# A hybrid decoder step: w_out, cq and co as seven half-size products, with the residual kept scaled and one weight queue behind the mixers

## The chip, the core and the metric

The kernel runs on one core of a Trainium2 chip. TensorE (PE) multiplies, VectorE (DVE) and ScalarE (ACT) do elementwise work, SyncE (SP) issues every DMA of this kernel, and GpSimd (POOL) does next to nothing. The metric is the device time of one launch in microseconds (us).

## The reference, cut to what matters

All is fp32. 512 prompt tokens and 8 decode tokens go through one layer with 2048 channels; both share the weights, so the kernel handles them as 520 columns.

```python
h  = rmsnorm(x, g_mix)
z  = h @ w_in                                   # 2048 -> 5128
y  = concat(rmsnorm(RG_LRU(z)) , headnorm(mLSTM(z)) * sigmoid(og))
x += y @ w_out
q  = rmsnorm(x, g_xattn) @ w_cq                 # 4 heads of 512
mk, mv = rmsnorm(mem, g_mem) @ w_mk, @ w_mv     # 256 memory tokens
x += softmax(q mk^T / sqrt(512)) mv @ w_co      # decode tokens: cached K, V of their own
x += relu(rmsnorm(x, g_ffn) @ w_up)^2 @ w_down  # 2048 -> 8192 -> 2048
out = rmsnorm(x, g_final)
```

## The kernel before

**Layout.** Channels lie on the 128 partitions and tokens in the columns: T is 520, HT half of it (260), and each activation is 16 tiles (k-tiles) of 128x520. Every fp32 product is three products of a shorter format: a weight is split into `whi` (a cast on ACT) and `wlo` (a subtraction on DVE), an activation likewise, and hi·hi, hi·lo and lo·hi are added in PSUM.

**The job list.** The mixers, w_out, w_cq, w_mk/w_mv and w_co are one list `jobs` of weight granules of 512 KB (8 k-tiles of 128x128). `run_jobs` takes them in order: job i+3 is loaded (`w_load`, L98), job i+2 is split (`w_split`, L105 on ACT, L106 on DVE), small generators in `tasks` are stepped by the job's cost, job i is multiplied (`gemm`, L157, 48 matmuls of 260 columns per granule), and its result is taken from PSUM. w_out, w_cq and w_co have 32 jobs each, so 1536 matmuls each; w_mk and w_mv have 64 together. Since the list runs on through all stages, the weights of the next stage are loaded and split while the one before still multiplies.

**Stages in the list.** `residual` (w_out and w_co) loads a tile of x (L699), adds the PSUM result (L705), stores the sum to DRAM (`dx`, L706), splits it as the operand of what follows (`xatt`), and adds up the squares; the norm itself is one row of factors (`rssx`, `rssf`) that is made behind the last tile by a small matmul (L208) and a Newton step (L198 to L201). `ev_q` (L726) multiplies the q tiles by that row. `attn_decode_all` is a task: per head and decode token it loads a broadcast q row and two K tiles of 256 KB, reduces them on DVE (L775), and later does the same with V (L802). It advances two steps per job in w_cq, and 0.7 steps in w_mk/w_mv (`DRATE` 2.0, `MCOST` 0.35). `attn_prompt` is started per head when its mk is there. Everything stays in SBUF, in 66 `slots`.

**Behind the list.** `ffn` closes all pools, and `prepare` loads x back, multiplies it by the norm (L1075, L1077), builds the eight column sums and halves that the fast product wants (`mixed`, L972 to L974), spills them to DRAM (L977), and reloads them as seven operand sets (`operand`, L983 to L986). From there each 2x2 block of weights (a unit: two output tiles, all of K in two halves) is done as **seven products of half size**, each of 24 matmuls of 260 columns (`product`, L1059) instead of eight. Four raw granules and three sums of them (L1025, four DVE operations) feed the seven products; each is split (L1040, L1041). There are 32 units for up and four groups (d1 to d4) of 8 for down; the results of up (L1093 to L1108) are spilled as the operands of down, and `down_evac` (L1118) adds products to x. At the end of a group the last unit frees one operand set per product and the next group's set is loaded and split into its place. Between up and down the weight pool is replaced, so no weight is loaded ahead there. The final norm stands at L1177 to L1193.

**Queues.** SP alone issues DMAs, in program order, and the DMAs take eight semaphores in turn, so a DMA also waits for the eighth one ahead of it. A DMA that waits for its data holds back all loads that stand behind it.

Of the kernel before, what the change touches and what calls it, by code (L numbers as in the profile page):

```python
# [19 lines left out]
NB = 8  # L20
# [7 lines left out]
SLOTS = 66  # L28
# [11 lines left out]
MCOST = 0.35  # L40
# [3 lines left out]
def tile_trunk(ctx: ExitStack, tc: tile.TileContext, a, o):  # L44
# [4 lines left out]
    keep = ctx.enter_context(tc.tile_pool(name="keep", bufs=1))  # L49
    part1 = ctx.enter_context(ExitStack())  # L50
    const = part1.enter_context(tc.tile_pool(name="const", bufs=1))
    slots = part1.enter_context(tc.tile_pool(name="slots", bufs=SLOTS))
    wpool = part1.enter_context(tc.tile_pool(name="wpool", bufs=3))
    small = part1.enter_context(tc.tile_pool(name="small", bufs=2))
    pmm = part1.enter_context(tc.tile_pool(name="pmm", bufs=2, space=PSUM))
# [35 lines left out]


# [8 lines left out]
    def w_split(i):  # L101
        raw = jobs[i].pop("raw")
        hi = wpool.tile([P, 8, P], F32R, tag="whi", name=nm("whi"))
        lo = wpool.tile([P, 8, P], F32R, tag="wlo", name=nm("wlo"))
        S.copy(hi, raw)  # L105
        V.tensor_tensor(out=lo, in0=raw, in1=hi.bitcast(F32), op=ALU.subtract)  # L106
        jobs[i]["w"] = hi, lo
# [141 lines left out]
    ident = const.tile([P, P], F32, name="ident")  # L249
# [11 lines left out]
    od = const.tile([P, 16, NB], F32, name="od")  # L261
    rmc = const.tile([P, 2], F32, name="rmc")
    rssf = keep.tile([P, T], F32, name="rssf")
    drows = dram.tile([4, 3, TP], F32, name="drows")

    st = {}
    xact, y = [], []
# [14 lines left out]
    def prologue():  # L282
# [9 lines left out]
        for k, x in enumerate(xs):  # L292
            g = pc(C_MIX, k)
            hi, lo = slot("xh", dt=F32R), slot("xl", dt=F32R)
# [18 lines left out]
    def rstd_task(key, n=D):  # L313
        yield
        st["r" + key] = rstd_of(st[key], n, "r" + key, rssf if key == "ssf" else None)
# [12 lines left out]
    def early_task():  # L328
        st["rssq"] = rstd_of(st["ssq"], D, "rssq")
        yield  # L330
        for ev, t in early:
            ev(halves(t))
# [156 lines left out]
    def ml_prompt(h):  # L489
# [102 lines left out]
        r = rstd_of(sq, 256, "rh")  # L592
        for j in range(2):
# [27 lines left out]
    def rnn(i, xc):  # L621
# [41 lines left out]
        if i == 7:  # L663
            yield
            yield
            rr = rstd_of(st["ssr"], 1024, "rr")
            for i in range(8):
# [4 lines left out]
                y.append(split(hg[i], "yr"))  # L672


    ym = []

    def ev_og(i):
        def ev(ps):
# [4 lines left out]
            ym.append(split(hm[i], "ym"))  # L683
            if i == 7:
                assert not tasks and len(y) == 8
                y.extend(ym)
# [62 lines left out]
    def attn_decode(h):  # L749
# [27 lines left out]
        for _ in range(4):  # L777
            yield
# [552 lines left out]
```

## Time and profile before

| | |
|---|---|
| median of three runs | 2898.87 us (2893.91, 2899.44, 2898.87) |
| the profiled execution | 2893.72 us, span 2892.0 us |
| mean granted TensorE clock | 0.973 |
| moved by DMA | 464.38 MB, 161 GB/s over the span |
| w_out on TensorE | 624.0 to 808.2 us |
| w_cq | 808.2 to 996.6 us |
| w_mk and w_mv with the attention | 996.7 to 1243.0 us |
| w_co | 1243.0 to 1433.4 us |
| gap with `prepare`, then up and down | 1433.4 to 1491.6 us, then to 2864.7 us |

The profile gives busy time per engine, and for each wait what ended it. A stage in which PE is busy all the time is bound by its matmuls; where PE is idle, the wait that ended last there is the price. A windows view gives, for a stretch of time, its length, the busy time of PE, PE weight loads, DVE, ACT and POOL with their instructions in brackets, the granted PE clock as a share of full speed, the busy share of the DMA engines, and GB/s.

### The profile page before, as it was taken

Reading aid. Unit: us, or ns where it says so; the run is one execution under the profiler, and the core shown is the slowest. Engines: PE = TensorE matmul, PEld = TensorE weight load, DVE = VectorE, ACT = ScalarE, POOL = GpSimd, SP = SyncE. Lnnn points to the kernel's source line nnn. Section 1 sums busy time; section 2 is a strip of 40 time slices with the busy share of each in tenths; the row PEclk is TensorE's granted clock in tenths of the full one; section 3 lists DMA queues with packets and bytes.
Section 4 is the critical chain, followed back from the end, with each engine's and each line's share of the span. In section 5 each row is a group of like instructions: output and inputs, shape, how many; then the busy total and the mean of one; then the engine's idle time right before and its main releaser. Section 6 shows DMA issues by size and latency. Waiting matters only on the chain.

```text
span 2892.0 us, 51735 instructions
## 1 busy us (share of the span) xinstructions
PE 2717.2 (94%) x21558; PEld 2662.7 (92%) x21558; DVE 2001.2 (69%) x3098; ACT 1225.0 (42%) x1620; POOL 31.3 (1%) x32
## 2 busy tenths in 40 slices
PE   7999999999999999999829999999998989999996
PEld 7999999999999988899829999999997989989896
DVE  7677687743346676733267777777778787887886
ACT  3444555632242244432225455454554343443543
POOL 3000000000000000000000000000000000000001
PEclk9999999999999999999959999999999999999998
DMA  4445442334448777744284544545456353433532
GB/s 149 144 164 169 163 140 86 96 103 139 135 152 269 271 250 253 227 139 133 91 291 161 163 160 156 168 141 169 154 183 224 102 191 110 155 139 109 190 106 81
DMA packets 198947, 464.38 MB, mean 161 GB/s; under 512 B 22349, under 2 KB 72173, under 8 KB 198713
## 3 DMA queue, kind: packets, MB, share of 16 engines
q1 hardware_dynamic: 198712, 461.08, 47.8%
q8 instruction: 169, 2.77, 0.4%
q14 instruction: 66, 0.53, 0.1%
HBM read 391.64 MB, written 69.49 MB: 159 GB/s over the span
## 4 chain that ended last, share of the span: by engine, by line
PE 77%; DMA 9%; DVE 9%; issue 2%; ACT 2%; SPq 1%; DVEq 0%; ACTq 0%
PE mm L157 29%; PE acca L1059 23%; PE accc L1059 12%; PE accb L1059 6%; PE mm L858 2%; DMA kv<-in_K 2%; PE aux L176 2%; DMA kv<-in_V 2%; PE mm L887 1%; DVE wlo L106 1%; DMA ct<-in_C 1%; DMA opl<-td 1%; DVE opl L986 1%; DVE wlo L1041 1%; DMA tdx<-w 1%
## 5 line engine op out<-in xcount | busy, mean ns | idle before, releaser
L1059 PE MATMUL acca<-oph,whi 128*128 128x260 f32 x2048 | 585.4, 286 | 63.6 <-ACT whi L1040 59.3
L1059 PE MATMUL acca<-opl,whi 128*128 128x260 f32 x2048 | 586.5, 286 | 13.5 <-DVE opl L986 13.1
L1059 PE MATMUL acca<-oph,wlo 128*128 128x260 f32 x2048 | 583.4, 285 | 3.2 <-DVE wlo L1041 3.0
L105 ACT CAST whi<-wraw 128x1024 fp32r<-128x1024 f32 x242 | 253.4, 1048 | 604.4 <-PE mm L157 382.8
L1059 PEld LDWEIGHTS acca<-oph,whi 128*128 128x128 f32 x2048 | 389.1, 190 | 66.7 <-ACT whi L1040 61.2
L106 DVE TENSOR_TENSOR wlo<-wraw,whi 128x1024 fp32r<-128x1024 f32 x242 | 298.2, 1233 | 189.7 <-ACT whi L105 187.8
L1059 PEld LDWEIGHTS acca<-opl,whi 128*128 128x128 f32 x2048 | 389.8, 190 | 17.1 <-DVE opl L986 17.1
L1040 ACT CAST whi<-raw 128x1024 fp32r<-128x1024 f32 x256 | 268.6, 1051 | 303.4 <-PE acca L1059 133.7
L1059 PEld LDWEIGHTS acca<-oph,wlo 128*128 128x128 f32 x2048 | 391.0, 191 | 4.4 <-DVE wlo L1041 4.3
L1041 DVE TENSOR_TENSOR wlo<-raw,whi 128x1024 fp32r<-128x1024 f32 x256 | 312.3, 1220 | 51.7 <-ACT whi L1040 51.3
L1040 ACT CAST whi<-raws 128x1024 fp32r<-128x1024 f32 x192 | 201.2, 1048 | 303.7 <-PE accc L1059 109.9
L1041 DVE TENSOR_TENSOR wlo<-raws,whi 128x1024 fp32r<-128x1024 f32 x192 | 234.7, 1222 | 114.3 <-ACT whi L1040 114.0
L1059 PE MATMUL accc<-oph,whi 128*128 128x260 f32 x1024 | 292.7, 286 | 5.6 <-ACT whi L1040 3.2
L1059 PE MATMUL accc<-oph,wlo 128*128 128x260 f32 x1024 | 291.5, 285 | 4.0 <-DVE wlo L1041 4.0
L1059 PE MATMUL accc<-opl,whi 128*128 128x260 f32 x1024 | 292.6, 286 | 0.8 <-DVE opl L986 0.6
L157 PE MATMUL mm<-xh,whi 128*128 128x260 f32 x1312 | 275.0, 291 | 10.9 <-DVE xh L295 10.7
L157 PE MATMUL mm<-xl,whi 128*128 128x260 f32 x1312 | 268.6, 286 | 5.6 <-DVE xl L296 5.5
L157 PE MATMUL mm<-xh,wlo 128*128 128x260 f32 x1312 | 268.9, 286 | 0.3 <-DVE wlo L106 0.3
L157 PEld LDWEIGHTS mm<-xh,whi 128*128 128x128 f32 x1312 | 207.5, 192 | 13.5 <-ACT whi L105 6.2
L157 PEld LDWEIGHTS mm<-xl,whi 128*128 128x128 f32 x1312 | 205.8, 191 | 7.8 <-DVE xl L296 7.8
L157 PEld LDWEIGHTS mm<-xh,wlo 128*128 128x128 f32 x1312 | 206.3, 192 | 0.7 <-DVE wlo L106 0.6
L1059 PEld LDWEIGHTS accc<-oph,whi 128*128 128x128 f32 x1024 | 194.4, 190 | 7.2 <-ACT whi L1040 4.4
(371 smaller groups left out, 5695.5 us busy)
## 6 DMA issues: line engine op xcount, KB each, us to landing
raw<-in_w_up SPq DMA_DIRECT2D x128, 512.0 KB
raw<-in_w_down SPq DMA_DIRECT2D x128, 512.0 KB
wraw<-in_w_in SPq DMA_DIRECT2D x80, 512.0 KB
td<-w SPq DMA_DIRECT2D x32, 1040.0 KB
opl<-td SPq DMA_DIRECT2D x56, 520.0 KB
wraw<-in_w_out SPq DMA_DIRECT2D x32, 512.0 KB
wraw<-in_w_cq SPq DMA_DIRECT2D x32, 512.0 KB
kv<-in_K SPq DMA_DIRECT2D x64, 256.0 KB
```

Source lines behind the costliest of these rows:

```text
L105: S.copy(hi, raw)
L106: V.tensor_tensor(out=lo, in0=raw, in1=hi.bitcast(F32), op=ALU.subtract)
L157: PE.matmul(ps[:, hf, 0:HT], w[:, j, :], x[:, HALF[hf]], start=(k == 0 and wi == 0), stop=(k == n - 1 and wi == 2))
L176: PE.matmul(out, u, v, start=first and i == 0, stop=last and i == 2)
L858: PE.matmul(box["ps"], w[:, i, :], x, start=(k == 0 and wi == 0), stop=(k == KB - 1 and wi == 2))
L887: PE.matmul(box["ps"][:, i], x[:, ms], w[:, j], start=(k == 0 and wi == 0), stop=(k == KB - 1 and wi == 2))
L986: V.tensor_tensor(out=lo, in0=lo.bitcast(F32), in1=hi.bitcast(F32), op=ALU.subtract)
L1040: S.copy(hi, raw)
L1041: V.tensor_tensor(out=lo, in0=raw, in1=hi.bitcast(F32), op=ALU.subtract)
L1059: PE.matmul(out, w[:, k], x[:, j], start=(new and k == 0 and i == 0), stop=(k == 7 and i == 2), skip_group_check=not new)
```

## The change

`rest` replaces everything behind the mixers, `ffn` among it.

- w_out, w_cq and w_co become 8 units each of seven half-size products, like up and down: 1344 matmuls each, not 1536. Their weights are packed in DRAM as w_up's (`pairs`). w_mk and w_mv keep their matmuls (`plain`, 64 granules).
- One list `seq` holds the products of all stages, and one weight queue (`sources`, `fetch`, `prep`, 7 raw tiles) runs through it, also from up to down: a product is prepared two ahead (`LOOK`).
- The operands of each product are seven sets with all sums, spilled to DRAM (`td`) as they are made and reloaded by `set_load`, a set as soon as the last unit of the stage before has freed its place. For the last of eight k-pairs `set_tail` splits straight from SBUF. The mixers spill theirs in `pair_out`.
- Norms move. The residual x is multiplied by the first norm's row (`scl`) in `scale_x` while the mixers run, and what is added to it carries the same factor, so that the norm of the attention is applied to q only (`r1`, and `esc` stands for the epsilon). The MLP needs none in front, since relu² scales with the square of its input: x is scaled back instead (`up_enter`, `scale_back`).
- The memory tokens' norm and gain are made in the mixers (`mem_prep`, to DRAM) and reloaded as w_cq's operand sets fall free (`mem_load`). q goes to DRAM and comes back per head in `attn_prompt`. K and V are packed for 512-KB loads with 4 KB per partition, where before 256 KB had 2 KB (K) or 1 KB (V) each.
- The decode attention is stepped 0.4 times per product of w_cq and twice per granule of w_mk and w_mv.
- `SLOTS` falls from 66 to 36.

The diff, cut to its core. First the mixers' side (`scale_x`, the factors, `pair_out`) and what the residual of before was:

```diff
+    def scale_x():
+        for n in range(KB):
+            x = slot("xs")
+            load(x, a["xT"][n])
+            yield
+            yield
+            V.tensor_tensor(out=x, in0=x, in1=scl, op=ALU.mult)
+            load(dx[0][n // 2][:, n % 2], x)
...
-        yield
+        st["rssq"] = rstd_of(st["ssq"], D, "rssq", scl)
+        V.scalar_tensor_tensor(out=esc, in0=scl, scalar=EPS, in1=scl, op0=ALU.mult, op1=ALU.mult)
+        yield
+        start(scale_x())
+        start(mem_prep(), 0.2)
...
+    def pair_out(k, ya, yb):
+        ta, tb = slot("ta"), slot("tb")
+        (a0, a1), (b0, b1) = ([t[:, c] for c in HALF] for t in (ya, yb))
+        (t1, t3), (t2, t4) = ([t[:, c] for c in HALF] for t in (ta, tb))
+        for out, in0, in1 in ((t1, a1, a0), (t3, b1, a1), (t2, b1, t1), (t4, b0, t2)):
+            V.tensor_tensor(out=out, in0=in0, in1=in1, op=ALU.subtract)
+        d = td["out"][k // 4]
+        load(d[:, 0:2, k % 4], halves(ya))
+        load(d[:, 4:6, k % 4], halves(ta))
+        load(d[:, 3, k % 4], b0)
+        load(d[:, 2, k % 4], b1)
+        load(d[:, 6:8, k % 4], halves(tb))
...
-    def residual(wname, acts, src, dst, gain, key, out):
...
-            def ev(ps, n=n, box=box):
-                if n == 0:
-                    st[key] = slot(key)
-                x1 = slot("x1")
-                V.tensor_tensor(out=halves(x1), in0=ps, in1=halves(box["x"]), op=ALU.add)
-                load(dst[n], x1)
-                if out is not None:
-                    out.append(split(x1, "xa", pc(gain, n)))
-                add_sq(st[key], x1, n == 0)
-                if n == KB - 1:
-                    start(rstd_task(key))
-            js += gemm([a[wname][n, g] for g in range(2)], acts, ev, pre)
-        return js
```

Then the core of `rest`: operand sets, the weight queue, the residual, q and the decode attention, the ends of the stages, and the loop over `seq` (what stood behind the last product of before, `final`, keeps its form):

```diff
+        def set_load(key, s, last=4):
+            out = []
+            for b, n in ((0, 4), (1, last)):
+                hi, lo = op_tile(), op_tile()
+                load(lo[:, 0:n].bitcast(F32), td[key][b][:, s, 0:n])
+                S.copy(hi[:, 0:n], lo[:, 0:n].bitcast(F32))
+                lo_of(lo[:, 0:n], lo[:, 0:n].bitcast(F32), hi[:, 0:n])
+                out.append((hi, lo))
+            sets[key, s] = out
+        def set_tail(key, j, wa, wb=None):
+            for _, _, s in ORDER:
+                src = wa[:, s] if wb is None or s < 4 else wb[:, s - 4]
+                hi, lo = sets[key, s][1]
+                S.copy(hi[:, j], src)
+                lo_of(lo[:, j], src, hi[:, j])
...
+        def fetch(k, q):
+            if k < len(sources):
+                t = praw.tile([P, 8, P], F32, tag="raw", name=nm("raw"))
+                load(t, sources[k][q])
+                raws[k, q] = t
+        def prep(n):
+            if n < len(seq):
+                ws[n] = split_weights(seq[n]["prep"]())
+        A11, A21, A22, A12, SS = range(5)
...
+        def strassen(key, n, src, evac, enter_=None, leave=None, left=None):
+            for u in range(n):
+                k = len(sources)
+                sources.append([src(u, i, j) for i, j in ((0, 0), (1, 0), (1, 1), (0, 1))])
+                box = {}
+                for p in range(7):
+                    job = dict(unit=k, q=p, cost=0.2, prep=lambda k=k, p=p: weights(k, p),
+                               run=lambda w, p=p, box=box: product(key, p, w, box),
...
+                    st_["w"] = w
+                    if u < 7:
+                        spill(nxt, u, w)
+                    load(dx[dst][u], X)
+                    if u == 0:
+                        st_["ss"] = tl("ss", (P, 2, T))
+                        S.activation(flat(st_["ss"]), flat(X), AF.Square)
+                    else:
+                        sq = tl("sq", (P, 2 * T))
+                        S.activation(sq, flat(X), AF.Square)
+                        V.tensor_tensor(out=flat(st_["ss"]), in0=flat(st_["ss"]), in1=sq, op=ALU.add)
...
+                V.tensor_tensor(out=t[:, 2], in0=t[:, 2], in1=r[:, 1], op=ALU.mult)
+                V.tensor_tensor(out=t[:, 3], in0=t[:, 3], in1=r[:, 0], op=ALU.mult)
+                h, j = u // 2, 2 * (u % 2)
+                d = dq32[h]
+                load(d[:, j], flat(t[:, 0:2]))
+                load(d[:, j + 1, 0:HT], t[:, 3])
+                load(d[:, j + 1, HT:T], t[:, 2])
...
+        def attn_decode(h):
...
+            def fetch(b, rows, n, src):
+                q, t = tl("qb", (P, 512)), tl("kv", (P, 1024))
+                load(q[:, 0:n], rows_of(rows, b * n, n))
+                load(t, src[h, b].rearrange("p a b -> p (a b)"))
+                return q, t
+            cur = [fetch(b, dqd[h], 512, a["K"]) for b in range(2)]
+            for b in range(NB):
+                yield
+                qb, kt = cur.pop(0)
+                for i in range(2):
...
+        def mem_load(s):
+            k4 = len(mact) // 4
+            if k4 < 4:
+                hi, lo = op_tile((P, 4, NMEM)), op_tile((P, 4, NMEM))
+                load(lo.bitcast(F32), dmem[:, 4 * k4:4 * k4 + 4])
+                S.copy(hi, lo.bitcast(F32))
+                lo_of(lo, lo.bitcast(F32), hi)
+                mact.extend((hi[:, j], lo[:, j]) for j in range(4))
...
+        def att_left():
+            while tasks:
+                step_tasks()
+            for _, _, s in ORDER:
+                set_load("co", s, 3)
+            set_tail("co", 3, *wlast)
...
+        def up_enter():
+            enter("d", t=2, w=2, x=2, r=1)()
+            v, s_ = tl("t", (P, 2, T))[:, 0], tl("t", (P, 2, T))
+            mean_of(v)
+            st["rphi"] = tl("r", (P, T))
+            V.reciprocal(s_[:, 0], v)
+            V.reciprocal(s_[:, 1], scl)
+            V.tensor_tensor(out=st["rphi"], in0=v, in1=s_[:, 1], op=ALU.mult)
+            V.tensor_tensor(out=scl, in0=scl, in1=s_[:, 0], op=ALU.mult)
+            start(scale_back())
...
+        def plain(srcs, run, post):
+            for q0 in range(0, len(srcs), 4):
+                k = len(sources)
+                sources.append(srcs[q0:q0 + 4])
+                for q in range(4):
+                    seq.append(dict(unit=k, q=q, cost=1.0, prep=lambda k=k, q=q: raws[k, q],
+                                    run=lambda w, g=q0 + q: run(g, w), post=lambda g=q0 + q: post(g)))
```

```diff
...
+        for n, j in enumerate(seq):
+            if "enter" in j:
+                j["enter"]()
             with tc.high_priority(offset=AHEAD):
...
+                if j["q"] < 4:
+                    fetch(j["unit"] + 1, j["q"])
+                prep(n + LOOK)
+            step_tasks(j["cost"])
+            j["run"](ws.pop(n))
...
```

**SP, from the mixers to w_out.** Rows give line, operation, what is written from what, and shape. Before, the weights of w_out (`wraw`) are loaded among those of the mixers, and its own evacuations come between them:

```order
L98 DMA wraw_6911<-in_w_in 128x1024
L98 DMA wraw_6973<-in_w_in 128x1024
L98 DMA wraw_7028<-in_w_out 128x1024
L98 DMA wraw_7090<-in_w_out 128x1024
L98 DMA wraw_7145<-in_w_out 128x1024
L98 DMA wraw_7207<-in_w_out 128x1024
L98 DMA wraw_7264<-in_w_out 128x1024
L98 DMA wraw_7327<-in_w_out 128x1024
L98 DMA wraw_7384<-in_w_out 128x1024
L706 DMA dx_0_100<-x_1002_7319 128x520
L699 DMA xr_7454<-in_xT 128x520
L98 DMA wraw_7448<-in_w_out 128x1024
```

Now the last pair of the mixers is spilled (`hh`, `ta`, `tb` to `tdout`), x is fetched for the first units, and the four raw weights of the first unit and the first operand set (`op`) stand behind that:

```order
L713 DMA tdout_109<-tb_7186 128x2x260
L709 DMA tdout_109<-hh_4081 128x2x260
L928 DMA x_7579<-dx_0_124 128x1040
L928 DMA x_7811<-dx_1_125 128x1040
L710 DMA tdout_109<-ta_7408 128x2x260
L711 DMA tdout_109<-hh_4082 128x260
L712 DMA tdout_109<-hh_4082 128x260
L713 DMA tdout_109<-tb_7409 128x2x260
L844 DMA raw_7446<-in_w_out 128x1024
L844 DMA raw_7448<-in_w_out 128x1024
L844 DMA raw_7450<-in_w_out 128x1024
L844 DMA raw_7452<-in_w_out 128x1024
L824 DMA op_7455<-tdout_108 128x1040
```

The loads that w_out begins with have moved from the mixers' stretch to behind the last head's spills, with the first operand set behind them.

**DVE, in the w_mk and w_mv stage.** Before, the decode attention's K reductions (L775) stand in some of the gaps between weight splits (`wlo`), with the prompt attention of a head (`mk`, `qa`) in others:

```order
L106 TENSOR_TENSOR wlo_11670<-wraw_11632,whi_11669 128x1024
L186 TENSOR_TENSOR mkl_11737<-mk_11519,mkh_11736 128x512
L106 TENSOR_TENSOR wlo_11701<-wraw_11667,whi_11700 128x1024
L775 ISA kv_11600,sc_11250<-kv_11600,kv_11599 128x512
L775 ISA sc_11250 128x1
L865 TENSOR_TENSOR mk_11664<-mm_11673,rm_9932 128x256
L775 ISA kv_11601,sc_11250<-kv_11601,kv_11599 128x512
L775 ISA sc_11250 128x1
L106 TENSOR_TENSOR wlo_11733<-wraw_11698,whi_11732 128x1024
L186 TENSOR_TENSOR mkl_11741<-mk_11664,mkh_11740 128x512
L186 TENSOR_TENSOR qal_11745<-q_9266,qah_11744 128x512
L106 TENSOR_TENSOR wlo_11780<-wraw_11730,whi_11779 128x1024
```

Now two K reductions (L1035; where V is due, four of L1054) stand in each gap:

```order
L98 TENSOR_TENSOR wlo_11796<-raw_11706,whi_11795 128x1024
L1035 ISA kv_11624,sc_11622<-kv_11624,qb_11623 128x512
L1035 ISA sc_11622 128x1
L1035 ISA kv_11624,sc_11622<-kv_11624,qb_11623 128x512
L1035 ISA sc_11622 128x1
L1095 TENSOR_TENSOR op_11566<-mk_11768,rm 128x256
L98 TENSOR_TENSOR wlo_11832<-raw_11750,whi_11831 128x1024
L1035 ISA kv_11628,sc_11622<-kv_11628,qb_11627 128x512
L1035 ISA sc_11622 128x1
L1035 ISA kv_11628,sc_11622<-kv_11628,qb_11627 128x512
L1035 ISA sc_11622 128x1
L818 TENSOR_TENSOR op_11836<-op_11566,op_11835 128x1024
```

Four splits of before have one pair of reductions among them, in their three gaps; now every gap has its pair, each on a load of 512 KB of its own and a broadcast row (`qb`).

**DVE, at the end of w_co.** Before, the last sum of squares (`ssf`) is followed by the norm's row (L209 to L201) and then `prepare` (L1075, L1077), with nothing of the next product between:

```order
L705 TENSOR_TENSOR x_2179_15902<-mm_15801,xr_15799 128x520
L220 TENSOR_TENSOR ssf_14267<-ssf_14267,sq_15905 128x520
L705 TENSOR_TENSOR x_2183_16007<-mm_15910,xr_15908 128x520
L220 TENSOR_TENSOR ssf_14267<-ssf_14267,sq_16010 128x520
L209 TENSOR_SCALAR rssfv_16013<-aux_16014 128x260
L209 TENSOR_SCALAR rssfv_16013<-aux_16017 128x260
L199 TENSOR_TENSOR rssft_16021<-rssfs_16020 128x520
L200 SCALAR_TENSOR_TENSOR rssft_16021<-rssft_16021,rssfv_16013 128x520
L201 SCALAR_TENSOR_TENSOR rssf<-rssft_16021,rssfs_16020 128x520
L1075 SCALAR_TENSOR_TENSOR w_16054<-xs_16051,par,rssf 128x260 x2
```

Now the splits of up's operand sets (L818: `op` from `op` for seven k-pairs, `op` from `w` for the last) and up's first weights (`wlo`, sums `raws`) stand among the last additions (`x`), and the two reciprocals of `up_enter` come between them:

```order
L818 TENSOR_TENSOR op_16085<-w_16241,op_16084 128x260
L798 TENSOR_TENSOR raws_16210<-raw_16089,raws_16210 128x1024
L818 TENSOR_TENSOR op_16123<-op_16123,op_16122 128x1040
L98 TENSOR_TENSOR wlo_16377<-raw_16006,whi_16376 128x1024
L818 TENSOR_TENSOR op_16128<-w_16241,op_16127 128x260
L961 SCALAR_TENSOR_TENSOR t_16298<-ax_16276,esc 128x260
L961 SCALAR_TENSOR_TENSOR t_16298<-ax_16279,esc 128x260
L1198 RECIPROCAL t_16299<-scl 128x520
L818 TENSOR_TENSOR op_16128<-op_16128,op_16127 128x780
L818 TENSOR_TENSOR op_16162<-op_16162,op_16161 128x1040
L818 TENSOR_TENSOR op_16167<-w_16241,op_16166 128x260
L1197 RECIPROCAL t_16299<-t_16298 128x520
```

The reload through a separate stage is gone; its place is taken by operand splits, weight splits and 520-column reciprocals in one row.

More of the change, by code (lines that the diff above doesn't have):

```diff
@@ L1198, in w_in @@
+        final()
+        stage["stack"].close()
+        whole.close()
     def w_in(n):
```

829 lines of the change are left out of this document (405 added, 424 removed).

## The prediction

> **What bounds the kernel now.** I read the page first: the share of each engine, and the share of the chain of waits that ended last.
>
> ```profile
> PE 2717.2 (94%) x21558; PEld 2662.7 (92%) x21558; DVE 2001.2 (69%) x3098; ACT 1225.0 (42%) x1620; POOL 31.3 (1%) x32
> PE 77%; DMA 9%; DVE 9%; issue 2%; ACT 2%; SPq 1%; DVEq 0%; ACTq 0%
> ```
>
> TensorE is busy for 94% of the span and holds 77% of the chain: matmuls bound the kernel, DMA and VectorE hold 9% each. Those are averages, so I cut the span by stage: mixers, w_out, w_cq, w_mk/w_mv, w_co.
>
> ```profile
> 45.00:624.00 579.00, 565.51 (x4540) 557.96 (x4539) 414.26 (x902) 288.05 (x460) 1.99 (x9) 0.98 0.40 129
> 624.00:808.20 184.20, 184.20 (x1538) 184.20 (x1537) 70.34 (x79) 52.12 (x64) 0.00 (x0) 1.00 0.42 136
> 808.20:996.60 188.40, 187.94 (x1564) 187.01 (x1564) 112.43 (x297) 56.03 (x83) 0.00 (x0) 1.00 0.69 229
> 996.70:1243.00 246.30, 232.29 (x1459) 206.57 (x1458) 175.06 (x428) 110.70 (x193) 0.00 (x0) 0.98 0.74 242
> 1243.00:1433.40 190.40, 190.40 (x1561) 188.90 (x1559) 60.12 (x69) 44.66 (x57) 0.00 (x0) 1.00 0.38 122
> ```
>
> In w_out, w_cq and w_co PE is busy without a gap, the clock is full, and VectorE has over 40% to spare. Fewer matmuls there are time saved, if VectorE and the loads keep up. The w_mk/w_mv stage is another matter: PE idles 14 us, VectorE is busy for 71%, DMA for 74%.
>
> **What goes.** Three stages lose 192 matmuls each, 576. The chain gives their price, and two rows of TensorE's timeline show the gap of `prepare`:
>
> ```profile
> 1254.67 178.78 PE mm L157 x1488
> 1433.03 0.40 PE L157 MATMUL mm<-oh,wlo 128*128 128x260 f32 x2
> 1491.57 0.58 PE L1059 MATMUL acca<-oph,whi 128*128 128x260 f32 x1 [54.68 <-ACT whi L1040]
> 1557.73 5.76 PE acca L1059 x48
> 2142.37 5.76 PE acca L1059 x48
> ```
>
> 178.78/1488 is 0.120 us, so 576 give **-69.2**. w_co ends at 1433.4, the first product starts at 1491.6: 58.1 us, all of which goes. A run of 48 on `acca` spans the border of two units; 29 borders from 1557.73 to 2142.37 make a unit 20.16 us. The first border seen begins the third unit at 1557.73 + 2.88 = 1560.6, so the first two took 69.0 us instead of 40.3: 28.7 more. Without `prepare`, **-86.8**. What its successor costs comes below. The profiled execution took 2893.7 us; 2893.7 - 69.2 - 86.8 = **2737.7**.
>
> **What comes: the transitions.** Each fast stage wants seven operand sets made, reloaded and split before its first unit. Two such borders stand in the trace, up to d1 and d3 to d4:
>
> ```profile
> 2222.74 5.81 PE acca L1059 x48
> 2668.94 4.25 PE acca L1059 x35
> 2740.86 5.76 PE acca L1059 x48
> ```
>
> From 2142.37 to 2222.74 lie three units and the border: 80.4 - 60.5 = 19.9. From 2668.94 to 2740.86, likewise, 71.9 - 60.5 = 11.4. Five borders now: mixers to w_out, w_out to w_cq, w_mv to w_co, w_co to up, up to down. What they must do on VectorE is in the groups by line:
>
> ```profile
> L1041 DVE TENSOR_TENSOR wlo<-raw,whi 128x1024 fp32r<-128x1024 f32 x256 | 312.3, 1220 | 51.7 <-ACT whi L1040 51.3
> L986 DVE TENSOR_TENSOR opl<-opl,oph 128x1040 fp32r<-128x1040 f32 x70 | 86.2, 1234 | 18.7 <-ACT oph L985 18.5
> L1025 DVE TENSOR_TENSOR raws<-raws,raw 128x1024 f32<-128x1024 f32 x64 | 78.3, 1224 | 1.7
> L1118 DVE TENSOR_TENSOR X<-acca,X 128x260 f32<-128x260 f32 x128 | 54.1, 423 | 27.6 <-PE acca L1059 27.6
> L972 DVE TENSOR_TENSOR w<-w 128x520 f32<-128x520 f32 x40 | 27.8, 694 | 2.1 <-ACT w L1108 1.8
> L231 DVE RECIPROCAL gs<-gs 4x520 f32<-4x520 f32 x1 | 3.4, 3391 | 0.0
> ```
>
> A first unit costs VectorE 7 weight splits (8.5 us), 4 sums (4.9), 14 operand splits (17.3) and 7 additions (3.0): 33.7, against a unit of 20.16. Operations in sequence overlap by about 0.08 us, so 31.
>
> - Mixers to w_out: no gap before. Now the last head's multiply, sigmoid, multiply and three subtractions (about 4 us by the rows of 0.69 for 520 and 0.42 for 260 columns), the spills, then four raw weights and two operand halves of 532 KB through SP before the first product: 3.2 MB, 8 to 9 us at the 358 to 414 GB/s shown below; with two transits of some 2 us and a cast and a split, the first product is about 18 late. The unit behind it adds 31 - 20 = 11, and a clock not yet full some 3: **+32** (20 to 50).
> - w_out to w_cq: sets are reloaded while the last unit runs, as in d3 to d4, and VectorE carries `mixed` and the tail splits more: **+16** (11.4 to 22).
> - w_mv to w_co: the last head's evacuation, split, 24 matmuls, `mixed`, and only then all seven sets: **+21** (15 to 35).
> - w_co to up: as w_out to w_cq, and two reciprocals of 520 columns on 128 partitions. The row has 4 partitions, 3.4 us; I take 3.4 each: **+22** (15 to 30).
> - Up to down: weights now run ahead, which brings 19.9 nearer to 11.4, while 16 tiles of x are still loaded there: **-5** (-10 to 0).
>
> **What comes: the attention.** Before, the 4 heads' decode steps are spread over w_cq and most of w_mk/w_mv. Now one half-head is done in w_cq, and the other steps come at two per granule: they end within the first 40 granules. Rows of the reductions, of a granule's matmuls and of the fastest and the mean load rate while K and V come:
>
> ```profile
> L802 DVE CUSTOM_DVE_ANT_0 kv<-kv,kv 128x256 f32<-128x256 f32 x128 | 48.3, 420 | 35.7 <-DMA kv<-in_V 35.1 <-issue 0.5
> L775 DVE CUSTOM_DVE_ANT_0 kv<-kv,kv 128x512 f32<-128x512 f32 x64 | 43.0, 688 | 43.8 <-DMA kv<-in_K 43.2 <-DVE sc L775 0.6
> 1069.42 19.90 PE mm L858 x168
> 860.00:1030.00 170.00, 163.77 (x1332) 162.14 (x1332) 104.66 (x290) 40.98 (x49) 0.00 (x0) 0.98 0.81 270
> 1000.00:1010.00 10.00, 7.66 (x61) 7.08 (x60) 7.10 (x17) 2.09 (x2) 0.00 (x0) 1.00 0.94 358
> 2160.00:2170.00 10.00, 8.55 (x70) 8.13 (x68) 6.10 (x8) 6.42 (x8) 0.00 (x0) 1.00 1.03 414
> ```
>
> For those 40 granules PE needs some 135 us (24 matmuls at 0.118 each is 2.84 a granule, w_mv's little less, and two heads' attention of 11). VectorE needs about 193: 40 splits 49, 48 K reductions 37 (with 0.08 to read each sum), some 120 of V 60, two heads' attention 35, the rest 12; 155 if all overlap. The loads up to the 40th granule's weights are, by the shapes, 68 MB (weights 20.5, K 12.6, V 14, broadcast rows 10, the rest 11): 165 us at 414 GB/s, 190 at 358, 252 at 270. So loads and VectorE bound this part, not PE. I take 203 us, or 336 GB/s, nearest to the row of 358. The last 24 granules hold two heads' prompt attention and take 88. Together 291 against 246: **+45** (10 to 95). The half-head in w_cq: **+3**.
>
> On this the Trainium skill, "Perfetto Trace Analysis", section Roofline, says that one core alone may draw more than its 358 GB/s share, up to about 435 from its 16 DMA engines. The trace agrees: 414 with the engines full. At 435, an estimate by that page, the loads would take 157 us, and VectorE's 155 to 193 would decide: rival 1.
>
> **The rest.** VectorE in a unit of w_out, w_cq and w_co needs about 19 of 20.16 us, so a late load shows at once: +3 (0 to 10). The mixers carry 21 us more of VectorE work, 40 spills on SP and the memory's norm, under a PE that idles 13 us in 579 already: +3 (0 to 20). Tail: +2.
>
> Sum: 32 + 16 + 21 + 22 - 5 + 45 + 3 + 3 + 3 + 2 = 142, so 2737.7 + 142 = **2880** in the profiled execution's terms. The runs lie 0.2 to 5.7 above its 2893.7; I add 4: **2884**, 15 below the median. Differences within 0.2%, 2893.1 to 2904.7, are no change here.
>
> **Rivals.**
> 1. The stage of w_mk/w_mv is not held by loads: its K and V now come in rows of 4 KB, like the operand sets that reached 414 GB/s. Then it costs +10, and with borders at their lower bounds (20, 11.4, 15, 15: 30 less) the time is 2884 - 35 - 30 = 2819; by the stage alone 2849. For it: 414 for 10 us. Against: a mean of 270 over 170 us with waits for K and V on VectorE of 79 us in all.
> 2. Slower: the same stage runs at the rate that the trace shows for K and V in the mean. 68 MB at 270 GB/s are 252 us, the stage 340, +94 instead of +45: **2933**. Every wait for K or V holds the weight splits behind it on VectorE, then PE. It decides from 224 us for the 40 granules, 304 GB/s: there the time passes 2904.7. For it: the kernel before reaches 270 with the DMA engines 0.81 busy and VectorE waiting, so the rate is one of waiting, not of capacity, and now more loads per granule stand on one SP; against: 512-KB loads, two ahead.
> 3. The change doesn't bring what it says, since VectorE takes PE's place in the 24 new units. At 1.5 us a unit that is +36, **2920**. Against it: up's 29 units at 20.16, none longer.
> 4. The clock. In the 60 us behind `prepare`'s gap it stays low:
>
> ```profile
> 1490.00:1500.00 10.00, 6.44 (x26) 5.63 (x26) 6.65 (x6) 4.44 (x6) 0.00 (x0) 0.60 1.02 414
> 1510.00:1520.00 10.00, 6.64 (x28) 5.74 (x27) 5.97 (x6) 3.24 (x4) 0.00 (x0) 0.50 0.44 161
> 1540.00:1550.00 10.00, 9.76 (x80) 9.55 (x80) 9.68 (x9) 6.45 (x9) 0.00 (x0) 1.00 0.17 54
> ```
>
> 0.50 at 1510 and full only at 1540, once PE is busy again: a starved unit runs slow as well. At borders mixers to w_out and w_mv to w_co, if 30 us each pass at 0.6, matmuls that fill 6 of 10 us stretch by some 7 each beyond my 3: 2884 + 14 = 2898. The Trainium skill, "TensorE: Matmul & The Clock Gate", Part 1, has the gate open after some 3.4 us of sustained work; by that alone a border would lose 1.7 us, an estimate by the page. The row at 1510 shows more, for work that isn't sustained.
>
> **Numbers.** Forecast, 2866 to 2904.7: 0.44, of which 0.12 at or above 2893.1. Rival 1, below 2866: 0.24. Rival 2: 0.23. Rival 3: 0.07. Rival 4 falls into the forecast's upper part: 0.02 beyond it. Faster 0.32 + 0.24 = 0.56, same 0.12, slower 0.32. Range 2838 to 2940: it leaves out the low half of rival 1 and the worst of rival 2, with about 0.1 each.
>
> **What would show it.** PE windows over w_out, w_cq and w_co: units at 20.2 us, each stage about 161 us plus its border; over 21.5 a unit speaks for rival 3. The w_mk/w_mv stage: 281 to 300 us, with VectorE waiting for `kv` or `qb`; under 260 rival 1, over 315 rival 2. Borders: gaps of PE in the first unit of 32, 16, 21, 22. The up to d0 border under 20. I am wrong if the mixers' stretch grows by over 20 us, which no row here prices.

## The result and the profile after

The change made the kernel **slower by 2.4%**: 2966.17 us (median of four runs, 2964.04 to 2970.31) against 2898.30 (four runs, 2893.91 to 2899.44), a ratio of 1.0239 with a 95% interval of 1.0221 to 1.0257. The forecast was 2884, the range 2838 to 2940. The profiled execution took 2964.66 us.

The page of the profile after, its span, busy times and chain:

```profile
span 2962.9 us, 51442 instructions
PE 2700.3 (91%) x20990; PEld 2626.2 (89%) x20990; DVE 2294.6 (77%) x3458; ACT 1344.3 (45%) x1759; POOL 31.3 (1%) x32
PE 66%; DVE 13%; DMA 12%; issue 4%; ACT 4%; SPq 1%; DVEq 0%; ACTq 0%; POOL 0%; POOLq 0%
```

The records hold 568 matmuls fewer (576 were meant to go), yet TensorE's busy time fell by only 17 us (2717.2 before), where 576 at 0.120 us are 69. Its share of the chain fell from 77% to 66%; DVE and DMA, 9% each before, took most of it. The core also moved more, 531.80 MB where it was 464.38, since the operands of three more stages are spilled and reloaded. The stages show where the time went. Windows view of the changed kernel, cut where the last matmul of a stage or the first of the next stands: w_out, w_cq, w_mk/w_mv, w_co, up, down (us, PE, PE weight loads, DVE, ACT, POOL, granted clock, DMA share, GB/s):

```profile
628.94:831.80 202.86, 173.56 (x1341) 170.05 (x1341) 163.29 (x196) 94.49 (x105) 0.00 (x0) 0.91 0.65 221
831.80:1023.60 191.80, 172.26 (x1375) 170.07 (x1374) 157.54 (x206) 92.24 (x126) 0.00 (x0) 0.94 0.57 192
1023.60:1365.70 342.10, 268.17 (x1482) 225.33 (x1480) 227.12 (x598) 107.28 (x164) 0.00 (x0) 0.89 0.78 257
1365.70:1566.00 200.30, 171.81 (x1342) 169.44 (x1341) 155.94 (x197) 90.11 (x106) 0.00 (x0) 0.90 0.61 204
1566.00:2237.90 671.90, 654.87 (x5390) 652.38 (x5390) 535.18 (x592) 346.67 (x439) 0.00 (x0) 0.98 0.55 174
2237.90:2933.80 695.90, 661.65 (x5378) 653.40 (x5376) 566.35 (x655) 299.79 (x312) 0.00 (x0) 0.99 0.41 140
```

| stage, us | before | forecast | after |
|---|---|---|---|
| to the end of the mixers | 624.0 | 627.0 | 628.9 |
| w_out | 184.2 | 194.1 | 202.9 |
| w_cq | 188.4 | 185.3 | 191.8 |
| w_mk/w_mv, to w_co's first product | 252.5 | 297.5 | 342.1 |
| w_co | 184.3 | 183.2 | 200.3 |
| `prepare` and up | 732.0 | 667.2 | 671.9 |
| down | 699.3 | 694.3 | 695.9 |
| end | 27.3 | 29.3 | 29.1 |
| sum | 2892.0 | 2878 | 2962.9 |

(Before, w_co's 1536 matmuls at 0.120 us are put at 184.3, and the rest of its stretch, the last head's attention, is counted with w_mk/w_mv. Forecast: the stage of before with the terms of the prediction.)

Of the 85 us between forecast and measurement, 45 lie in the w_mk/w_mv stage, 32 at the borders of w_out, w_cq and w_co. The gain of `prepare` came as forecast. The waits view of the changed kernel between 1023.6 and 1263.8 us, the stretch in which the decode attention runs (engine, line, what it waited for: us in total, times, longest):

```profile
ACT whi L97 <- DMA raw<-in_w_mv: 52.9, 12, 7.7
ACT whi L97 <- DMA raw<-in_w_mk: 47.8, 12, 19.7
...
PE mk L1087 <- ACT whi L97: 24.3, 4, 14.6
...
DVE kv L1035 <- DMA kv<-in_K: 17.9, 11, 3.5
```

The weights come late (101 us of waits of ScalarE's cast `whi`), then PE waits for the cast. For the same stretch, the waits of SP's queue:

```profile
SPq L1025 <- DVE od L1054: 35.8, 19, 3.0
SPq L1025 <- DVE sc L1035: 27.5, 12, 2.8
SPq L1047 <- DVE pd L1011: 20.5, 3, 7.4
SPq L1025 <- DMA qb<-dp: 20.3, 10, 4.8
```

SP, which also loads the weights, stands before loads of decode rows (`qb`, L1025) until a reduction frees their buffer. This reads like a queue that is blocked at its head; the experiments show that it isn't the cause.

### The profile page after: what moved, and what is told of

Same layout as the page of the kernel before. It is cut to its first block, busy times and chain, and to the rows that moved or that the text cites. A ratio compares the mean times of both kernels' runs of the same rounds, so it can differ in the third digit from the quotient of the medians.

```text
span 2962.9 us, 51442 instructions
## 1 busy us (share of the span) xinstructions
PE 2700.3 (91%) x20990; PEld 2626.2 (89%) x20990; DVE 2294.6 (77%) x3458; ACT 1344.3 (45%) x1759; POOL 31.3 (1%) x32
## 2 busy tenths in 40 slices
DMA packets 224645, 531.80 MB, mean 179 GB/s; under 512 B 23692, under 2 KB 97132, under 8 KB 224408
## 4 chain that ended last, share of the span: by engine, by line
PE 66%; DVE 13%; DMA 12%; issue 4%; ACT 4%; SPq 1%; DVEq 0%; ACTq 0%; POOL 0%; POOLq 0%
PE acca L900 30%; PE accc L900 15%; PE mm L162 9%; PE accb L900 8%; DVE wlo L98 3%; DVE op L818 2%; DMA qb<-dp 1%; ACT whi L97 1%; DMA op<-tdd 1%; PE mv L1110 1%; DMA raw<-in_w_mv 1%; PE ax L181 1%; DVE raws L798 1%; DMA kv<-in_V 1%; PE mk L1087 1%
## 5 line engine op out<-in xcount | busy, mean ns | idle before, releaser
L900 PE MATMUL acca<-op,whi 128*128 128x260 f32 x5632 | 1051.3, 286 | 82.5 <-ACT t L918 20.2
L900 PEld LDWEIGHTS acca<-op,whi 128*128 128x128 f32 x5632 | 881.8, 190 | 92.0 <-DVE op L818 24.2
L900 PE MATMUL acca<-op,wlo 128*128 128x260 f32 x2816 | 804.1, 286 | 4.1 <-DVE wlo L98 3.9
L900 PEld LDWEIGHTS acca<-op,wlo 128*128 128x128 f32 x2816 | 537.4, 191 | 5.0 <-DVE wlo L98 4.9
L900 PE MATMUL accc<-op,whi 128*128 128x260 f32 x2816 | 524.2, 284 | 11.3 <-DVE op L818 7.6
L162 PE MATMUL mm<-xa,whi 128*128 128x260 f32 x2624 | 439.8, 289 | 21.3 <-ACT ssq L321 7.3
L900 PEld LDWEIGHTS accc<-op,whi 128*128 128x128 f32 x2816 | 439.5, 190 | 14.6 <-DVE op L818 9.8
L900 PE MATMUL accc<-op,wlo 128*128 128x260 f32 x1408 | 399.6, 284 | 0.7 <-DVE wlo L98 0.7
L162 PEld LDWEIGHTS mm<-xa,whi 128*128 128x128 f32 x2624 | 370.6, 192 | 26.1 <-DVE xa L310 7.4
L900 PE MATMUL accb<-op,whi 128*128 128x260 f32 x1408 | 272.3, 292 | 28.3 <-DVE op L818 16.7
L818 DVE TENSOR_TENSOR op<-op,op 128x1040 fp32r<-128x1040 f32 (+2 forms) x132 | 156.6, 1190 | 26.6 <-ACT op L825 18.1
```

What stands on the lines that cost most here:

```text
L162: PE.matmul(ps[:, hf, 0:HT], w[:, j, :], x[:, HALF[hf]], start=(k == 0 and wi == 0), stop=(k == n - 1 and wi == 2))
L818: V.tensor_tensor(out=lo, in0=src, in1=hi.bitcast(F32), op=ALU.subtract)
L900: PE.matmul(out, u[:, k], x[:, j], start=(new and k == 0 and i == 0), stop=(k == 7 and i == 2), skip_group_check=not new)
```

## The experiments

Stages are compared, since the chips differ: the kernel before took 2886.9 on the chip of the first four runs (`a_`), and 2898.5, 2890.9, 2894.8 (median) and 2892.4 on those of `b_`, `c_`, `d_` and `e_`. Every run but `d_` is a single execution beside a single one of the kernel before. The change's stage of w_mk/w_mv, 342 us, and its borders are the reference; in `a_late_sets`, which leaves that stage alone, it is 342 again. The "theories" are named in the texts that say what was expected.

### What holds the w_mk/w_mv stage

Without the decode loads:

```diff
...
-                load(q[:, 0:n], rows_of(rows, b * n, n))
-                load(t, src[h, b].rearrange("p a b -> p (a b)"))
-                return q, t
+                return st["still"]
```

> The changed kernel without the decode attention's loads of K, V and their broadcast rows (the reductions run as before, on tiles of zeros; the decode columns' result is left out). The w_mk/w_mv stage, from the end of w_cq to the first product of w_co, took 341 us. Theory 1 (loads: the amount at some 275 GB/s, or their waits in SP's queue): the stage falls to 255 to 280 us, the time to about 2880 to 2905. Theory 2 (VectorE's reductions between the weight splits hold the stage): it stays above 320 us, the time above 2945.

2879.95 us, ratio 0.998 to the kernel before on that chip. Windows view of the stage in this run:

```profile
1022.10:1269.20 247.10, 237.41 (x1481) 208.03 (x1480) 209.94 (x534) 107.38 (x162) 0.00 (x0) 0.99 0.62 202
```

The stage is 247 us, PE busy for 237 of them: bound by matmuls again. All of the 95 us hang on the loads, with the waits for their data and their buffers.

The reductions made short, all loads kept:

```diff
-                    t = kt[:, i * 512:(i + 1) * 512]
+                    t = kt[:, i * 512:i * 512 + 8]
...
```

> The changed kernel with all loads, but each reduction over 8 columns, where it was 512 or 256 (the decode columns' result is left out): about 70 us of VectorE work less in the w_mk/w_mv stage. Theory 1 (the amount of bytes): the stage stays at 330 to 345 us, the time at 2955 to 2968. Theory 2 (VectorE's reductions): it falls by 40 us or more, to 300 or less. Theory 3 (waits in SP's queue for buffers that VectorE frees): between, 310 to 330.

2959.79 us, the stage 330:

```profile
1021.70:1351.80 330.10, 263.23 (x1482) 223.41 (x1480) 174.03 (x591) 107.35 (x164) 0.00 (x0) 0.89 0.78 266
```

VectorE's busy time falls from 227 to 174 us, the stage by 12 of the 95. Its work isn't what holds the stage.

The decode loads on another queue:

```diff
-                load(q[:, 0:n], rows_of(rows, b * n, n))
+                G.dma_start(out=q[:, 0:n], in_=rows_of(rows, b * n, n))
```

and likewise K, V and the softmax's store.

> The changed kernel with the decode attention's loads (K, V, broadcast rows) and the store of its softmax issued by GpSimd, not SP: same bytes, same reductions, another queue. Theory 1 (the amount of bytes at the chip's rate): the stage stays above 325 us. Theory 3 (SP's queue: weights stand behind loads that wait for buffers, and behind the softmax's store): the stage falls to 285 to 310 us, the time to 2910 to 2935, and the rate in it rises above 290 GB/s.

2964.72 us, the stage 341. Four rows of this run's waits view, over 1022 to 1300 us:

```profile
POOL qb L1025 <- DVE od L1054: 82.2, 24, 12.1
DVE kv L1054 <- DMA qb<-dp: 47.3, 24, 6.5
...
PE mv L1110 <- DVE wlo L98: 24.6, 9, 6.1
...
PE mk L1087 <- DVE wlo L98: 17.8, 9, 6.9
```

The weights no longer stand behind the decode loads, but VectorE now waits for the rows, GpSimd for VectorE, and TensorE for the weight splits `wlo` that stand behind the reductions on VectorE: the stage is as long as before. **The head of SP's queue was a symptom.** The reading that is left is that the time of a decode step counts, from its loads to its reduction; the next runs shorten it.

Three steps ahead, not two:

```diff
-            enter("b", t=3, kv=3, qb=2, r=1, sm=1)()
+            enter("b", t=3, kv=3, qb=3, r=1, sm=1)()
...
-            cur = [fetch(b, dqd[h], 512, a["K"]) for b in range(2)]
+            cur = [fetch(b, dqd[h], 512, a["K"]) for b in range(3)]
...
```

V is treated alike.

> The changed kernel with three steps' loads of K or V and row ahead, not two (three row buffers, not two): same bytes. Theory 4 (two loads in flight, some 10 us from issue to reduction, give 5 us a step): the stage falls by 40 us or more. Theory 1 (the rate of all loads, DMA engines 0.83 busy): within 12 us of 342.

2944.36 us, the stage 321: 21 less, between the two forecasts.

Half of each K and V load:

```diff
-                load(t, src[h, b].rearrange("p a b -> p (a b)"))
+                load(t[:, 0:512], src[h, b].rearrange("p a b -> p (a b)")[:, 0:512])
...
```

> The changed kernel with half of each K and V load (256 KB, 2 KB per partition; the reductions do the same amount on the loaded half, the decode columns' result is left out): 13 to 14 of 68 MB less. Theory 1 (bytes): the stage 45 to 60 us shorter. Theory 4 (number of steps and their latency): 10 to 25 us shorter.

2924.79 us, the stage 301: 41 less for 13 to 14 MB, short of what theory 1 expected and well over theory 4.

K and V loaded, their broadcast rows not:

```diff
...
-                load(q[:, 0:n], rows_of(rows, b * n, n))
...
-                return q, t
+                return st["still"], t
```

> The changed kernel without the broadcast rows' loads (256 KB for K, 128 KB for V, each the same row for all partitions; the reductions use a tile of zeros, the decode columns' result is left out); K and V are loaded. Theory 1 (bytes at 275 GB/s): 10 of 68 MB less, the stage 30 to 45 us shorter. Theory 4 (the chain of a step: reduction, free buffer, row, reduction): 50 us or more shorter. If neither, under 20.

2884.68 us, and the stage is 257:

```profile
1022.50:1279.70 257.20, 239.44 (x1481) 209.50 (x1480) 210.08 (x532) 107.20 (x162) 0.00 (x0) 0.98 0.81 283
```

85 of the 95 us are gone with some 10 of 68 MB, while K and V, 27 MB, still come. The rows cost far more than their bytes: 10 MB at the stage's 257 GB/s would be some 39 us. Two runs took that apart. In the first the rows have places of their own in DRAM and nothing to wait for, in the second one row serves all partitions and nothing is waited for:

```diff
-                load(q[:, 0:n], rows_of(rows, b * n, n))
+                load(q[:, 0:n], src[h, (b + 4) % NB].rearrange("p a b -> p (a b)")[:, 0:n])
```

> The changed kernel with the broadcast rows' loads replaced by loads of the same size whose partitions read places of their own (the head of another decode token's K or V; nothing to wait for; the decode columns' result is left out). Without these loads the w_mk/w_mv stage fell from 342 to 257 us. Theory R1 (128 partitions read one row, and that is slow): the stage stays near that, 255 to 280 us. Theory R2 (10 MB in short packets, whatever their place): 320 us or more. Theory R3 (rows come late behind the softmax's store and the queries' store): as R1 here, told apart by the next run.

```diff
...
-                load(q[:, 0:n], rows_of(rows, b * n, n))
+                load(q[:, 0:n], rows_of(still, b * n, n))
```

> The changed kernel with the broadcast rows taken from a DRAM tensor that is written once at the start of w_cq: still one row for all 128 partitions, the same bytes, but no wait for the softmax's or the queries' store (the decode columns' result is left out). Theory R1 (one row for all partitions is slow): the stage stays at 325 us or more. Theory R3 (the rows' own waits): 255 to 285 us. Theory R2: 320 us or more.

2921.61 and 2943.68 us. The stage with rows apart, and, in the fence behind it, with rows free:

```profile
1016.90:1316.00 299.10, 253.94 (x1481) 216.96 (x1480) 214.74 (x534) 106.52 (x161) 0.00 (x0) 0.93 0.79 274
```

```profile
1026.60:1341.50 314.90, 258.72 (x1482) 220.95 (x1480) 215.60 (x534) 107.27 (x162) 0.00 (x0) 0.90 0.77 260
```

342, 315, 299, 257: of the rows' 85 us, some 27 are the wait for the stores that make them, 16 that all partitions read one place, 42 that they are loaded at all, when they are taken away in this order. No run tried another order. None of R1 to R3 explains it alone.

The decode steps at the pace of before:

```diff
-                    job = dict(unit=k, q=p, cost=0.2,
+                    job = dict(unit=k, q=p, cost=0.57 if key == "cq" else 0.2,
...
-                    seq.append(dict(unit=k, q=q, cost=1.0,
+                    seq.append(dict(unit=k, q=q, cost=0.35,
```

> The changed kernel with the decode attention stepped at the pace of before: 1.14 steps per product of w_cq (0.4 in the change) and 0.7 per granule of w_mk/w_mv (2 in the change). Theory 1 (loads crowded into the first 40 granules hold the stage of 342 us, while w_cq moves 192 GB/s with the DMA engines 0.56 busy): the stage falls by 50 to 75 us, w_cq grows by 5 to 20, the time falls by 35 to 60 against the changed kernel's 2954 or so on this chip. Rival (both stages together are at the limit of the loads): w_cq grows by as much as the other falls, the time within 15 us.

2907.89 us, ratio 1.003. w_cq and the stage behind it in this run:

```profile
828.30:1041.00 212.70, 181.56 (x1386) 176.87 (x1385) 175.47 (x313) 90.95 (x129) 0.00 (x0) 0.92 0.66 219
1041.00:1301.70 260.70, 236.49 (x1455) 209.76 (x1453) 203.07 (x483) 107.80 (x157) 0.00 (x0) 0.95 0.85 299
```

81 us less in the one, 21 more in the other. All loads and waits are there, rows too, and in this run the kernel takes only 0.3% more than the one before. The two stages carry the decode steps when they aren't crowded into one: **the pace was the mistake in it**, and rows, waits and K/V are what a step is made of.

### What holds the borders

A border is what a stage takes beyond its eight units. In the changed kernel w_cq's first unit holds a gap of PE; so does w_co's. Two rows of its TensorE timeline, the first from w_cq, the second from w_co:

```profile
865.80 0.59 PE L900 MATMUL acca<-op,whi 128*128 128x260 f32 x1 [13.68 <-ACT t L918]
...
1410.42 0.80 PE L900 MATMUL acca<-op,whi 128*128 128x260 f32 x2 [14.05 <-DVE x L907]
```

It is the second product on bank a that waits: it adds to what the first left there, and the first must be taken out before, in w_cq by a copy on ScalarE (L918), in w_co by an addition to x on VectorE (L907). ScalarE's timeline of the same kernel shows what the copy stands behind:

```profile
859.09 1.06 ACT L825 CAST op<-op 128x1040 fp32r<-128x1040 f32 x1 [4.06 <-DMA op<-tdcq]
...
862.61 0.84 ACT L825 CAST op<-op 128x780 fp32r<-128x780 f32 x1
863.47 1.28 ACT L202 ACT_TABLE_LOAD   x1
864.84 0.64 ACT L202 ACTIVATE t<-t 128x520 f32<-128x520 f32 x1
865.39 0.36 ACT L918 COPY t<-acca 128x260 f32<-128x260 f32 x1
```

The splits of all seven sets and the norm's row come before the first copy. ScalarE itself waits there, 4.06 us in the first row, for the load of a set. So the sets were split later:

```diff
...
+            for m in seq[n:n + LOOK]:
+                if "set" in m:
+                    set_split(*m["set"])
             j["run"](ws.pop(n))
```

> The changed kernel with each operand set still loaded at its old place, but split only two products ahead of its use, so that the evacuations of a first unit's products no longer stand behind the splits of all seven sets on ScalarE and VectorE. Borders now: mixers to w_out 40 us, w_out to w_cq 27, w_mv to w_co 39, w_co to up 26, up to down 19, between the down groups 9 to 13. Theory A (the fifth product waits for an evacuation that stands behind all the splits): the first units' gaps of 14, 14 and 6.5 us shrink to under 4 and the five borders lose 30 to 50 us in sum. Theory B (the sum of VectorE's work in the first unit, 31 us, sets the border wherever it stands): within 10 us of before. Theory C (the sets' loads set it): no change, or slower by up to 15.

2946.03 us, ratio 1.0205. w_out, w_cq and w_co in this run:

```profile
625.60:816.90 191.30, 165.50 (x1344) 163.64 (x1344) 163.01 (x196) 92.50 (x103) 0.00 (x0) 0.95 0.69 235
816.90:1007.90 191.00, 172.57 (x1371) 169.83 (x1371) 158.40 (x207) 92.44 (x126) 0.00 (x0) 0.95 0.57 192
...
1349.90:1535.30 185.40, 168.32 (x1345) 166.83 (x1343) 155.09 (x196) 88.34 (x105) 0.00 (x0) 0.94 0.66 221
```

w_out is 12 us shorter, w_co 15, where all seven sets are loaded at once; w_cq is as long, up 2 and down 11 us longer, where the sets had come one by one. The gaps shrank to 10 and 11 us, not to under 4, and with the longer stages taken off some 14 us were won in all, not 30 to 50. Theory A holds for two borders and in part. In w_co the addition that ends the gap waits, last of all, for the load of x itself; the first row is from the change, the second from the run with late splits:

```profile
1409.94 0.43 DVE L907 TENSOR_TENSOR x<-acca,x 128x260 f32<-128x260 f32 x1 [0.56 <-DMA x<-dx]
...
1380.34 0.43 DVE L920 TENSOR_TENSOR x<-acca,x 128x260 f32<-128x260 f32 x1 [1.52 <-DMA x<-dx]
```

Whether an earlier load of x would shorten this border was not tried.

With the sets' loads on GpSimd's queue:

```diff
-                load(lo[:, 0:n].bitcast(F32), td[key][b][:, s, 0:n])
+                G.dma_start(out=lo[:, 0:n].bitcast(F32), in_=td[key][b][:, s, 0:n])
```

> The changed kernel with the operand sets' loads (14 per border) issued by GpSimd, not by SP between the raw weights; nothing else moved. Theory Q (the set loads stand in SP's queue behind raw weights that wait for a free buffer, which a weight split frees that itself stands behind the sets): the five borders, 152 us in sum, fall by 35 us or more, the three that lie between the four down groups with them. Theory B (VectorE's 31 us in the first unit): within 10 us of 152. Theory L (the loads' amount, 7.4 MB per border): within 15 us.

2965.58 us, ratio 1.025: w_out 204, w_cq 190, w_co 198, up 674, down 704. Theory Q falls. The low clock has its part in the borders. Two windows of the changed kernel, in w_cq's and in w_co's first unit:

```profile
845.00:866.00 21.00, 5.94 (x25) 5.44 (x26) 15.48 (x20) 12.15 (x18) 0.00 (x0) 0.53 0.59 218
1380.00:1396.00 16.00, 8.52 (x44) 8.01 (x44) 8.54 (x10) 5.07 (x7) 0.00 (x0) 0.62 0.50 190
```

Over the whole of the changed kernel's w_out, w_cq and w_co PE is busy for 173.6, 172.3 and 171.8 us, which is 13, 7 and 11 us more than their recorded matmuls take at 0.120 us each. What of the rest is VectorE's and ScalarE's work in order, the amount of the loads or their lateness wasn't taken apart.

### A version that beats both

The pace of before, and the sets of w_out and w_co split two products ahead of their use. The edit also moves the splits of the other sets a little: they come one product after the set's load, where the change has them directly behind it. It ran once, then four times more:

> Both remedies in one: the decode steps at the pace of before (stage 261, w_cq 213 us) and the operand sets of w_out and w_co split two products ahead of use (12 and 15 us less at these borders; w_cq, up and down as in the change). If the two add up, 2907.9 - 27 = 2881 on a chip whose kernel before takes 2898, which is faster than before by some 0.6%. If VectorE's work, once moved, comes back in the units behind, 2895 to 2905.

> The version with both remedies again, timed in rounds against the kernel before: by its first run (2857.8 against 2890.9) a ratio of 0.986 to 0.992, faster than both kernels. If the first run was a lucky one, 0.995 to 1.0.

2857.84 us beside 2890.88, then 2857.49 (four runs, 2856.93 to 2859.31) beside 2894.79: a ratio of **0.9871, interval 0.9854 to 0.9887**, 1.3% less than the kernel before. Its stages, w_out to w_co, in the second run:

```profile
623.00:814.90 191.90, 165.14 (x1328) 163.23 (x1329) 162.72 (x195) 93.11 (x104) 0.00 (x0) 0.94 0.69 234
814.90:1025.30 210.40, 182.31 (x1390) 177.87 (x1389) 176.32 (x316) 91.38 (x130) 0.00 (x0) 0.92 0.65 221
1025.30:1294.10 268.80, 242.69 (x1479) 213.74 (x1478) 206.26 (x491) 108.47 (x160) 0.00 (x0) 0.96 0.83 291
1294.10:1478.50 184.40, 166.37 (x1339) 164.80 (x1338) 155.09 (x195) 88.95 (x106) 0.00 (x0) 0.94 0.67 220
```

More came than the 27 us expected: down, too, is 17 us shorter than in the change (679). The moved splits of its sets are the only part of the edit that touches down, but no run has them alone, so that stays a guess. Adding the third edit, the sets' loads on GpSimd's queue, undid part of the gain:

> Pace of before, late splits, and the sets' loads on GpSimd's queue. The first two gave a ratio of 0.987 to the kernel before. If theory Q holds and adds to the late splits: 0.972 to 0.980. If the late splits had already taken what the queue costs: 0.984 to 0.990.

2867.22 beside 2892.41, 0.991: in this one run worse than without.

## Why the prediction was wrong

1. **What goes** was right. Three times 192 matmuls at 0.120 us: in their steady part the units take 20.2 us in w_co, 20.4 in w_out and 20.4 to 21.0 in w_cq. `prepare` and up fell from 732.0 to 671.9, where 667.2 was forecast.
2. **The step that failed** is in the attention's term, the rate of its loads: "I take 203 us, or 336 GB/s, nearest to the row of 358". The 40 granules took 240 us, at 269 GB/s; the windows view of the changed kernel, for them and for the 24 behind:

```profile
1023.60:1263.80 240.20, 171.26 (x937) 143.09 (x935) 159.69 (x492) 60.13 (x94) 0.00 (x0) 0.85 0.83 269
1263.80:1365.70 101.90, 96.92 (x545) 82.24 (x545) 67.44 (x109) 47.16 (x71) 0.00 (x0) 0.97 0.66 227
```

269 GB/s, the mean of before (270), though K and V now come in rows of 4 KB. That is rival 2: a rate of waiting. Its price for the stage, 340 us against 342 measured, is partly luck: it had 252 us for the 40 granules (240 came, since by this row 65 MB were moved, not 68) and 88 for the 24 behind (102 came). The row for it was in the prediction, a mean over 170 us in which K and V came as well; I chose a window of 10 us over it, and the only reason given was "512-KB loads, two ahead". K and V make up 27 of 68 MB; the broadcast rows and the stores that they wait for had stayed as they were, and I had counted the rows as 10 MB of bytes only. The runs put 85 of the stage's 95 us on them. The crowding was seen and priced as bytes and VectorE work, not as steps that each wait: at the pace of before, the stage takes 261 us.

3. **The borders were too cheap.** With w_out's, w_cq's and w_co's stages of eight units (161.3 us) taken off, they cost 42, 31 and 39 us, where the terms (1 for late loads each, and 3 for decode steps in w_cq) gave 33, 24 and 22 (w_cq with the 4 us that its stage held beside its 1536 matmuls before). The sum of VectorE's work in a first unit, 31 us, was taken as if products could run beside it. The timeline shows that they can't all: the second product on a bank waits for a copy or an addition that stands in order behind the splits of the sets of products still to come. Late splits gave back 12 and 15 us at two borders; the longer busy time of PE, at the low clock, is in them with 13, 7 and 11 us; the rest is open. Up (27) and up to down (19 against 15) were nearer; the reciprocals took 3.39 us each, as chosen.
4. **Rival 1** needed the stage to be free of its loads; without decode loads it is 247 us, where rival 1 had 256, so its price was near and its condition wrong. **Rival 3** fell: no steady unit is over 21.0, and its sign was 21.5. **Rival 4** came about at the borders: 10 us each at w_out and w_co by its terms (3 and 7), 13 and 11 by the busy times. It reached further: the clock granted in the w_mk/w_mv stage was 0.89, and the same matmuls kept PE busy for 268 us there, 237 in the run without decode loads. The change's mean is 0.953, before 0.973.
5. The **range** ended at 2940, below what the terms' own upper bounds give together; it left out the worst of rival 2 and took the errors of stage and borders as if they didn't meet. Here they did: the stage came at 90 us over before (its bound was 95), and the borders of w_cq and w_co, 31 and 39, passed their bounds of 22 and 35.

## What to carry to other kernels

When a stage gets shorter, ask what used to hide in it: the attention's loads and reductions lay beside w_cq's matmuls, and the new pace crowded them into the stage behind. Take the rate of a stage from the longest stretch in which the same mix of transfers ran, not from its best 10 us, and look at the smallest loads on the path of a step, which can cost far more than their bytes. At a border, write down what stands in order ahead of the first copy or addition out of PSUM.

## What was not expected of the hardware

A row that all 128 partitions read from one place is slower by the packet. In the traces, over the w_mk/w_mv stage, packets of 2 KB took 0.129 us in the mean in the change, 0.114 in the run with rows free (still one place for all partitions) and 0.099 in the run with rows apart; packets of 1 KB took 0.070, 0.063 and 0.049. Both sizes include some stores. Packets of 4 KB took 0.182 to 0.184 in all three. So only a part of the change's longer packets is the shared place; the rest was gone where the rows wait for no store, and no run says how the two hang together.

In this trace a TensorE that waits over and over is granted a lower clock: 0.85 in the mean over the 240 us of the 40 granules, in which it was busy for 171, against 0.97 over the 102 us behind, in which it was busy for 97.
